# Streaming logsumexp: the last two tiles are loaded and computed by one written list

## The chip, the cores and the metric

The kernel runs on one core of one Trainium2 chip. The metric is the device time of one execution in microseconds; the median of three runs of the kernel before is 323.24. The profile pages and traces come from one profiled execution each. Engines are named as in the profile: PE (TensorE), DVE (VectorE), ACT (ScalarE), POOL (GpSimd) and SP (SyncE, which only issues transfers here).

## The reference

```python
# x: (8, 2048, 2048) float32, bias: (8, 256) float32
x_heads = x.reshape(B, S, H, Dh).transpose(0, 2, 1, 3) + bias[None, :, None, :]
x_tiled = np.repeat(x_heads, 2, axis=2)
mx = x_tiled.max(axis=-1, keepdims=True)
lse = mx.squeeze(-1) + np.log(np.exp(x_tiled - mx).sum(axis=-1))
```

So each row of 2048 numbers has 8 heads of 256. For each row and head the kernel needs log(sum(exp(x + bias))), and writes it twice. The input is 134 MB, the output 1 MB.

## The kernel before

The 16,384 rows are cut into 64 tiles of 128 partitions by 2 rows (K = 2), 2 MB each. Eight tile buffers stand in SBUF (four `xb` of two tiles). SP issues all loads of x and later three of the four stores; a load may also have to wait until the eighth transfer before it has landed, since eight semaphores are used in turn. No maximum is subtracted: the sums of exp(x + bias) are taken directly, and a range check at the end decides whether a second, slow pass with the maximum (`all_again`) is run.

There are three ways to bring the bias in:

- PE: a matmul writes the bias of a head into a PSUM bank (bf16, L343 and L360), a second one with an identity matrix adds x (float32, L378 in `add_x`, L401). ACT then takes exp from PSUM and sums it by its accumulator (`sum_biased`, L432).
- ACT takes exp(x) in place (`exp_inplace`, L457), and DVE multiplies by exp(bias) and sums in one instruction (`weigh`, L492).
- ACT takes exp(x), and POOL multiplies by exp(bias) and folds 256 columns to 32 by three additions (`fold`, L508 and L516); DVE reduces the rest (L522).

In the bulk (tiles 0 to 53) POOL adds the bias of the upper heads instead (L451) and DVE reduces with L476. `STAGES` says which heads go which way from which tile on. Tiles 57 to 61 have two heads on PE, five on DVE, one on POOL, for each row by itself. Tile 62 has one on PE, six on DVE and one on POOL in each row; tile 63 has two, four and two in its first row and three, five and none in its second. Tile 63 is loaded in pieces of columns (`LAST_COLS`), and two pieces of its second row by one transfer (`LAST_BOTH`).

Every engine runs its instructions in the written order (`tc.manual_schedule`). The loop writes for each unit: the x-add on PE, the next unit's bias matmul, warm matmuls that nobody reads (`keep_warm`, L392), the exp, then the previous unit's sums from PSUM, then the weighing. So the sums of a unit stand behind the exp of the next one on ACT.

The end: all sums of the last batch stand in the tile `R_last`. PE transposes it (L696), ACT takes the log (L702) and issues the store (L703). The range check looks at the float bits of all sums as integers. Per group of batches DVE takes a maximum and a minimum and hands them on to the next group (`ends_of`, `ends_of_last(0)`, L563 and L564, between tiles 61 and 62), at the end it does so for the rest (`ends_of_last(1)`), combines both (L608), PE turns the 128 partitions into one row (L602, L616), DVE reduces that row to one number (L617), and every engine loads it into a register (L620) and branches.

Of the kernel before, what the change touches and what calls it, by code (L numbers as in the profile page):

```python
# [17 lines left out]
K = 2  # L18
# [18 lines left out]
PROMPT_F2 = dict(pe=2, acc=2, g0=8, late=False, fold=2)  # L37
SINGLE_F1 = dict(pe=1, acc=1, g0=8, late=False, fold=1)
TRIPLE = dict(pe=3, acc=3, g0=8, late=False, fold=0)
# [12 lines left out]
    (62, (SINGLE_F1, SINGLE_F1)),  # L52
    (63, (PROMPT_F2, TRIPLE)),
]

LAST_COLS = [
    [(0, 512), (1280, 2048), (512, 1280)],
    [(0, 512), (768, 1280), (1280, 1792), (512, 768), (1792, 2048)],
]

LAST_BOTH = (512, 1792)
# [3 lines left out]
def kernel(  # L65
# [41 lines left out]
    one_bits = sb.tile([1, 1], BF16, name="one_bits")  # L107
    ends = sb.tile([P, 2], F32, name="ends")
    far = sb.tile([P, 1], BF16, name="far")
    verdict = sb.tile([1, 1], I32, name="verdict")  # L110

    NR = KB * H * NB
# [6 lines left out]
    pads = [1] * (len(widths) - 1) + [NBLK * K]  # L119
# [10 lines left out]
    R.append(sums_in[-2].rearrange("p (k h n) -> p k h n", k=K, h=H))  # L130
    R_last = sums_in[-1].rearrange("p (h n k) -> p h n k", h=H, n=NBLK)
# [19 lines left out]
    def pieces(t):  # L151

        if len(modes_of(t)) == 1:
            return [(0, K, 0, D)]
        cols = [[(0, D)]] * K if t < T - 1 else LAST_COLS
        return [(k, k + 1, c0, c1) for k in range(K) for c0, c1 in cols[k]]
# [35 lines left out]
    def load(t):  # L192
        if TB <= t < BLOCKS:

            if t % TB == 0:
                after = [u for i in range(TB) if t >= NBUF for u in last_uses[t + i - NBUF]]
                ins = on_x(
                    t,
                    nc.sync.dma_start(
                        out=xbs[t // TB % len(xbs)], in_=rows_of(t, TB)  # L200
                    ),
                    after,
                )
                for i in range(TB):
                    loads[t + i, 0, 0] = ins
            return
        after = last_uses[t - NBUF] if t >= NBUF else []
        for k0, k1, c0, c1 in pieces(t):
            if t == T - 1 and k0 == K - 1 and c0 in LAST_BOTH:
                if c0 == LAST_BOTH[0]:  # L210
                    both = slice(0, None, (LAST_BOTH[1] - c0) // Dh)
                    v = [
                        a[:, k0, c0:D].rearrange("p (a j) -> p a j", j=Dh)[:, both]
                        for a in (xts[t % NBUF], rows_of(t))
                    ]
                    ins = on_x(t, nc.sync.dma_start(out=v[0], in_=v[1]), after)
                    for c in LAST_BOTH:
                        loads[t, k0, c] = ins
                continue
            loads[t, k0, c0] = on_x(  # L220
                t,
                nc.sync.dma_start(
                    out=xts[t % NBUF][:, k0:k1, c0:c1],
                    in_=rows_of(t)[:, k0:k1, c0:c1],
                ),
                after,
            )

    def reload(t):

        n = t + NBUF
        if n < BLOCKS:
            if n % TB == TB - 1:
                load(n - TB + 1)
        elif n < T:
            load(n)

# [50 lines left out]
    nc.vector.memset(Rx[-1], 1.0)  # L288
    nc.vector.memset(one_bits, float(ONE_BITS))
# [32 lines left out]
    def on_bank(i, ins):  # L322
        for j, u in bank_users[i // 2]:
            if j != i and u.ins.engine != ins.ins.engine:
                tc.declare_no_dep(ins.ins, u.ins, reason="another bank")
        bank_users[i // 2].append((i, ins))
        return ins
# [176 lines left out]
    def fold(t, k, h0, h1, sums, after):  # L504


        v = xts[t % NBUF][:, k, h0 * Dh : h1 * Dh]
        done = nc.gpsimd.tensor_tensor(  # L508
            out=v, in0=v, in1=w_sb[:, h0 * Dh - W1 : h1 * Dh - W1], op=ALU.mult
        )  # L510
        on_x(t, done, [after])
        v = v.rearrange("p (h j) -> p h j", j=Dh)
        n = Dh
        while n > FOLD:
            n //= 2
            done = nc.gpsimd.tensor_tensor(  # L516
                out=v[:, :, 0:n], in0=v[:, :, 0:n], in1=v[:, :, n : 2 * n], op=ALU.add
            )
            on_x(t, done, [])

        def add_fold():
            red = nc.vector.tensor_reduce(  # L522
                out=sums[:, k, h0:h1],
                in_=v[:, :, 0:FOLD],
                op=ALU.add,
                axis=mybir.AxisListType.X,
            )
            on_x(t, red, [done])

        return add_fold  # L530
# [29 lines left out]
    def min_max(low_in, high_in, low, high, axis, last=False):  # L560


        nc.vector.tensor_reduce(out=high, in_=high_in, op=ALU.max, axis=axis)  # L563
        nc.vector.tensor_reduce(out=low, in_=low_in, op=ALU.min, axis=axis, negate=last)  # L564

    def ends_of(i):


        bits = Rx[i].bitcast(I32)
        at = pads[i + 1] + widths[i + 1]  # L570
        min_max(
            bits[:, 0 : 1 + widths[i]],
            bits[:, 1:],
            Rx[i + 1][:, 0:1].bitcast(I32),
            Rx[i + 1][:, at : at + 1].bitcast(I32),
            mybir.AxisListType.X,
        )

    def ends_of_last(half):


        bits = Rx[-1].bitcast(I32)
        n = NBLK * K
        c = half * n // 2
        views = [
            bass.AP(
                tensor=bits.tensor,
                offset=bits.offset + c0 + c,
                ap=[bits.ap[0], [n, H + 1], [1, n // 2]],
            )  # L590
            for c0 in (0, n)
        ]
        if half == 0:
            c = n // 2
            to = [bits[:, c0 + c : c0 + c + 1] for c0 in (0, n + NR)]
        else:
            to = [ends[:, 0:1], ends[:, 1:2]]
        min_max(*views, *to, mybir.AxisListType.XY, last=half == 1)

    def begin_row():  # L600
        row = one_ps[0:1, 0:P]
        nc.tensor.matmul(row, lhsT=one_bits, rhs=ones_bf[0:1], start=True, stop=False)  # L602
        return row

    def judge(row):


        nc.vector.scalar_tensor_tensor(  # L608
            out=far,
            in0=ends[:, 1:2],  # L610
            scalar=-2.0 * ONE_BITS,
            in1=ends[:, 0:1],
            op0=ALU.add,
            op1=ALU.max,
        )
        nc.tensor.matmul(row, lhsT=far, rhs=ident_bf, start=False, stop=True)  # L616
        nc.vector.tensor_reduce(  # L617
            out=verdict, in_=row, op=ALU.max, axis=mybir.AxisListType.X
        )
        return nc.values_load(  # L620
            verdict,
            min_val=0,
            max_val=(1 << 31) - 1,
            skip_runtime_bounds_check_because="it is only compared, and addresses nothing",
        )

    def all_again():
# [10 lines left out]
        with tc.For_i(0, B, 1) as b, tc.For_i(0, S // P, 1) as n:  # L638
# [28 lines left out]
            nc.sync.dma_start(  # L667
# [41 lines left out]
    def sums_of(t):  # L709
# [16 lines left out]
        for t in range(T)  # L726
        for k0, k1, c0, _ in pieces(t)
        if c0 == 0
# [8 lines left out]
    for t in range(T):  # L737
# [4 lines left out]
        for k0, k1, c0, c1 in pieces(t):  # L742
# [3 lines left out]
            if c0 == 0:  # L746
                bias_here = bias_there
# [9 lines left out]
            if c0 == 0:  # L757
                if next_units and not m["late"]:
                    bias_there = put_bias(*next_units.pop(0))
                if t > T_PROMPT and m["g0"] == H:  # L760
                    keep_warm()
                if m["g0"] < H:
                    add = g_add(m, t, k0, k1)
                wait_for_pool = t == T_ROWS and k0 == 0
                if (t < T - 1 or k0 == 0) and not wait_for_pool:
                    flush(for_pool)
            h0 = max(c0 // Dh, m["pe"])
            h1 = min(c1 // Dh, m["g0"])
            hf = max(h0, min(h1, H - m["fold"]))
# [8 lines left out]
            if c0 == 0:  # L778
                flush(for_pe)
# [18 lines left out]
            if m["g0"] < H:  # L798
                pe_part()
                if t == T_PROMPT - 1:  # L800
                    first_factors()
                if m["late"]:
                    bias_there = put_bias(*next_units.pop(0))
            elif heads:
                for_pe.append(pe_part)
# [14 lines left out]
    flush(for_pe)  # L820
    flush(for_pool)
    finish_last()
    ends_of_last(1)
    again = judge(row) > SPAN_BITS
# [34 lines left out]
```

## Time and profile before

| | us |
|---|---|
| runs | 323.17, 323.24, 323.34 |
| the profiled execution | 323.2 |
| its span, first to last instruction | 321.3 |
| DVE busy | 287.8 (90%) |
| POOL busy | 288.2 (90%) |
| ACT busy | 264.4 (82%) |
| PE busy | 247.4 (77%) |
| moved by DMA | 135.44 MB, mean 422 GB/s |

The span is what the trace covers; the rest of the time lies around it. A row of the timeline gives the start, the length, the engine, the line of the kernel, the operation with output and input, and in brackets how long the engine was idle before it and what ended that. Engines overlap the end of one instruction with the start of the next, so costs in a row are read from start to start. A float32 matmul shows as two passes (x2).

### The profile page before, as it was taken

The page shows a single profiled execution, that of the slowest core. Times are in us where ns is not written, and L with a number is a line of the kernel's source. Part 1 is how long each engine was busy: PE and PEld are TensorE (multiplying, and loading weights), DVE is VectorE, ACT ScalarE, POOL GpSimd, SP SyncE. Part 2 cuts the span into 40 slices and gives each one's busy share as a digit, 9 for nine tenths or more (in the row PEclk, how much of TensorE's full clock was granted, in tenths as well). Part 3 has the DMA queues.
Part 4 walks back from the last instruction along what each step waited for, and adds up shares of the span by engine and source line. Part 5 has one row for each costly group of instructions (what it writes and reads, how often), then busy time and mean ns, then how long its engine had stood idle before and what let it go on. Part 6 is the DMA issues. An engine that isn't in the chain of part 4 may idle for free.

```text
span 321.3 us, 2277 instructions
## 1 busy us (share of the span) xinstructions
PE 247.4 (77%) x609; PEld 99.3 (31%) x610; DVE 287.8 (90%) x313; ACT 264.4 (82%) x434; POOL 288.2 (90%) x121
## 2 busy tenths in 40 slices
PE   4998885877886667887877876877877688688874
PEld 1333332323332223333323322332332233133331
DVE  1437999799989999969999999899999999999996
ACT  1159987798688888599789988889888998999995
POOL 6949998999999999999999999999999999978774
PEclk9979996899799999598999998999999999799999
DMA  7999999999999999999999999999999999999994
GB/s 297 455 424 453 416 438 443 404 457 432 416 457 413 432 451 412 441 445 408 450 438 420 445 414 436 424 428 428 439 434 426 425 424 446 415 424 429 428 410 183
DMA packets 8790, 135.44 MB, mean 422 GB/s; under 512 B 964, under 2 KB 1351, under 8 KB 2375
## 3 DMA queue, kind: packets, MB, share of 16 engines
q1 hardware_dynamic: 8624, 135.14, 98.3%
q10 hardware_dynamic: 152, 0.14, 0.1%
q8 instruction: 5, 0.08, 0.1%
q14 instruction: 9, 0.07, 0.1%
HBM read 134.23 MB, written 1.05 MB: 421 GB/s over the span
## 4 chain that ended last, share of the span: by engine, by line
DMA 48%; DVE 29%; PE 9%; ACT 8%; POOL 4%; issue 0%; SPq 0%; DVEq 0%
DMA xb<-in_x_dram 48%; DVE R L476 23%; ACT xb L457 5%; POOL xb L451 4%; DVE xb L469 4%; PE pair L401 4%; PE one_ps L401 2%; DVE xb L492 2%; PE pair L274 1%; ACT xb L419 1%; PE pair L343 1%; DMA brow<-in_bias_dram 1%; PE one_ps L343 1%; ACT xb L412 0%; PE w_ps L274 0%
## 5 line engine op out<-in xcount | busy, mean ns | idle before, releaser
L451 POOL TENSOR_TENSOR xb<-xb,b_rep 128x2048 f32<-128x2048 f32 x57 | 257.6, 4544 | 18.4 <-DMA xb<-in_x_dram 18.3
L476 DVE TENSOR_REDUCE R<-xb 128x14 f32<-128x3584 f32 (+1 forms) x57 | 216.8, 3803 | 2.6 <-ACT xb L457 0.7
L457 ACT ACTIVATE xb<-xb 128x2560 f32<-128x2560 f32 (+7 forms) x77 | 156.2, 2040 | 19.2 <-POOL xb L451 18.8
L401 PE MATMUL pair<-xb,ident 128*128 128x512 f32 x216 | 109.8, 634 | 0.0
L401 PE MATMUL one_ps<-xb,ident 128*128 128x512 f32 x108 | 62.9, 667 | 16.8 <-DMA xb<-in_x_dram 16.8
L419 ACT ACTIVATE xb<-pair 128x1024 f32<-128x1024 f32 x54 | 55.5, 1028 | 17.2 <-PE pair L401 17.1
L401 PEld LDWEIGHTS pair<-xb,ident 128*128 128x128 f32 x216 | 44.7, 207 | 58.7 <-issue 58.7
L469 DVE TENSOR_TENSOR xb<-xb,w_ps 128x512 f32<-128x512 f32 x54 | 36.7, 680 | 20.4 <-ACT xb L457 20.3
L343 PE MATMUL one_ps<-b,ones_bf 128*128 128x512 bf16 x52 | 19.9, 382 | 38.4 <-ACT xb L412 38.4
L412 ACT ACTIVATE xb<-one_ps 128x256 f32<-128x256 f32 x108 | 39.9, 378 | 7.0 <-PE one_ps L401 7.0
L343 PEld LDWEIGHTS <-ones_bf 128*128 128x128 bf16 (+1 forms) x174 | 17.4, 101 | 86.3 <-issue 79.3
L343 PE MATMUL pair<-b,ones_bf 128*128 128x512 bf16 x104 | 31.0, 379 | 0.0
L378 PE MATMUL pair<-xb,ident 128*128 128x512 f32 (+1 forms) x42 | 22.7, 636 | 9.5 <-DMA xb<-in_x_dram 9.5
L401 PEld LDWEIGHTS one_ps<-xb,ident 128*128 128x128 f32 x108 | 19.8, 200 | 31.5 <-DMA xb<-in_x_dram 25.3
L492 DVE CUSTOM_DVE_ANT_0 xb<-xb,w_ps 128x256 f32<-128x256 f32 x61 | 22.3, 416 | 0.0
L412 ACT ACTIVATION_READ_ACCUMULATOR xb<-one_ps 128x1 f32 x108 | 22.0, 204 | 0.0
L516 POOL TENSOR_TENSOR xb<-xb 128x128 f32<-128x128 f32 (+3 forms) x39 | 13.9, 356 | 3.1
L432 ACT ACTIVATE xb<-pair 128x256 f32<-128x256 f32 x39 | 14.7, 401 | 0.0
L508 POOL TENSOR_TENSOR xb<-xb,w_sb 128x256 f32<-128x256 f32 (+1 forms) x13 | 10.0, 772 | 4.9 <-ACT xb L457 4.4
L378 PEld LDWEIGHTS pair<-xb,ident 128*128 128x128 f32 x42 | 6.9, 195 | 21.2 <-DMA xb<-in_x_dram 19.2
L392 PE MATMUL tp<-b_rep,ident 128*128 128x384 f32 x28 | 11.3, 486 | 0.0
L492 DVE CUSTOM_DVE_ANT_0 xb<-xb,one_ps 128x256 f32<-128x256 f32 x21 | 8.5, 414 | 0.4 <-ACT xb L457 0.2
(61 smaller groups left out, 73.8 us busy)
## 6 DMA issues: line engine op xcount, KB each, us to landing
xb<-in_x_dram SPq DMA_DIRECT2D x20, 4096.0 KB, 21.9
xb<-in_x_dram SPq DMA_DIRECT2D x17, 2048.0 KB, 22.2
xb<-in_x_dram SPq DMA_DIRECT2D x12, 1024.0 KB, 22.3
xb<-in_x_dram SPq DMA_DIRECT2D x5, 256.0 KB, 11.1
xb<-in_x_dram SPq DMA_DIRECT2D x2, 384.0 KB, 15.6
out_dram<-res SPq DMA_DIRECT2D x1, 512.0 KB, 6.4
out_dram<-res SPq DMA_DIRECT2D x1, 256.0 KB
out_dram<-res_two SPq DMA_DIRECT2D x1, 128.0 KB, 5.7
```

Of the source, the lines that this page charges most:

```text
L343: nc.tensor.matmul(p, lhsT=lhsT, rhs=each_row(b, h * Dh, Dh, K), start=i == 0, stop=False,)
L378: mm = nc.tensor.matmul(p, lhsT=ident, rhs=xts[t % NBUF][:, ka:kb, c : c + w], start=False, stop=True,)
L401: mm = nc.tensor.matmul(p, lhsT=ident, rhs=xts[t % NBUF][:, :, h * Dh : (h + 1) * Dh], start=False, stop=True,)
L412: act = nc.scalar.activation(out=xts[t % NBUF][:, k, 0:Dh], in_=got[0][:, k * Dh : (k + 1) * Dh], func=ACT.Exp, accum_out=sums[:, k, 0:1],)
L419: act = nc.scalar.activation(out=xts[t % NBUF][:, :, Dh : m["pe"] * Dh].rearrange("p k (h j) -> p h k j", j=Dh), in_=got[-1].rearrange("p ...
L432: act = nc.scalar.activation(out=xts[t % NBUF][:, k, h * Dh : (h + 1) * Dh], in_=p, func=ACT.Exp, accum_out=sums[:, k, h : h + 1],)
L451: add = nc.gpsimd.tensor_tensor(out=v, in0=v, in1=each_row(b_rep, c - G0, D - c, k1 - k0), op=ALU.add)
L457: return on_x(t, nc.scalar.activation(out=v, in_=v, func=ACT.Exp), [after])
L469: mul = nc.vector.tensor_tensor(out=f, in0=f, in1=each_row(w_ps, m["pe"] * Dh - W0, n, k1 - k0), op=ALU.mult,)
L476: red = nc.vector.tensor_reduce(out=sums[:, k0:k1, h0:H], in_=v.rearrange("p k (h j) -> p k h j", j=Dh), op=ALU.add, axis=mybir.AxisListTy ...
L492: ttr = nc.vector.tensor_tensor_reduce(out=v, in0=v, in1=w, scale=1.0, scalar=0.0, op0=ALU.mult, op1=ALU.add, accum_out=dst,)
L516: done = nc.gpsimd.tensor_tensor(out=v[:, :, 0:n], in0=v[:, :, 0:n], in1=v[:, :, n : 2 * n], op=ALU.add)
```

## The change

Tiles 62 and 63 leave the stages and the loop. Their four rows get names: a and b are the rows of tile 62, c and d those of tile 63. A list (`TAIL_LOADS`) says which heads of which row each of ten transfers brings, and a second list (`TAIL`) writes the work on them in order, one word for each instruction: `add` (x onto the bias in PSUM, and the bias matmul of the next `add` behind it), `warm`, `exp`, `weigh`, `sum` (exp from PSUM with the accumulator), `copy` (exp of three heads from PSUM to SBUF, no sum), `halves` (DVE adds the two halves of such a head and sums, 128 elements), `fold` by single steps and `folded`. The sums of tile 61 (`sums`) stand ahead of the first exp of row a. The exps are 256 to 1280 elements for 256 to 1792 before.

The range check changes: POOL subtracts the bits of 1.0 from all sums that are known by tile 61 (`bits`), DVE reduces their absolute values to one number for each partition (`limit`), and at the end DVE does the same for the 32 last columns, with that number beside them; a matmul by a column of 2^-8 adds up the 128 partitions, and one element is copied. A constant column with the limit itself makes the sum exceed half the limit only if a partition does. In `all_again` a store is issued by ACT instead of SP.

```diff
-    (62, (SINGLE_F1, SINGLE_F1)),
-    (63, (PROMPT_F2, TRIPLE)),
 ]
+T_TAIL = 62
+TAIL_LOADS = [
+    (62, 0, 0, 8),
+    (62, 1, 4, 8),
+    (63, 0, 3, 8),
+    (63, 1, 4, 8),
+    (63, 0, 0, 1),
+    (62, 1, 2, 4),
+    (62, 1, 0, 2),
+    (63, 0, 1, 3),
+    (63, 1, 2, 4),
+    (63, 1, 0, 2),
+]
+ROWS = {"a": (62, 0), "b": (62, 1), "c": (63, 0), "d": (63, 1)}
+TAIL = """
+add a:01  sums  add a:2  warm  warm
+exp a:3-5  exp a:67
+weigh a:3  rest  weigh a:4  weigh a:5  weigh a:6  weigh a:7
+bits
+exp b:4-7
+fold b:67.0
+weigh b:4  weigh b:5
+copy a:012
+halves a:0  halves a:1  halves a:2
+exp c:3-7
+fold b:67.1
+limit
+add c:0  warm
+weigh c:3  weigh c:4
+exp d:4-7
+fold c:67.0
+weigh c:5
+add b:2
+exp b:3
+weigh d:4
+sum c:0
+weigh d:5
+add b:0  warm
+exp b:1
+fold c:67.1
+weigh d:6
+sum b:2
+add c:1  warm
+weigh d:7
+exp c:2
+fold b:67.2
+weigh b:3
+sum b:0
+add d:2
+weigh b:1
+exp d:3
+fold c:67.2
+weigh c:2
+sum c:1
+add d:0
+exp d:1
+weigh d:3
+fold b:67.3
+sum d:2
+weigh d:1
+fold c:67.3
+folded b:67
+sum d:0
+folded c:67
+"""
...
+    def next_bias():
...
+        p = ps[bank][:, 0:n]
+        mm = nc.tensor.matmul(
+            p, lhsT=ones_bf, rhs=each_row(b3, heads[0] * Dh, n, 1), start=True, stop=False
+        )
...
+        if what == "add":
+            bank, c = biased[(t, k), heads[0]]
+            mm = nc.tensor.matmul(in_ps(bank, c, n), lhsT=ident, rhs=v, start=False, stop=True)
+            on_bank(bank, on_x(t, mm, [loads[t, k, heads[0] * Dh]]))
...
+            next_bias()
...
+        if what == "copy":
+            bank, c = biased[(t, k), heads[0]]
+            act = nc.scalar.activation(out=v, in_=in_ps(bank, c, n), func=ACT.Exp)
...
+        if what == "halves":
+            (h,) = heads
+            ttr = nc.vector.tensor_tensor_reduce(
+                out=v[:, 0 : Dh // 2],
+                in0=v[:, 0 : Dh // 2],
+                in1=v[:, Dh // 2 :],
...
+                accum_out=dst,
+            )
...
+    def off_one(engine, to, bits):
+        engine.tensor_scalar(
+            out=to,
+            in0=bits,
+            scalar1=-1.0 * ONE_BITS,
+            scalar2=None,
+            op0=ALU.add,
+        )
...
+    def off_seen():
+        n = 1 + 2 + NR
+        off_one(nc.gpsimd, off[:, 1:n], Rx[len(groups)].bitcast(I32))
+        to = off[:, n:].rearrange("p (h c) -> p h c", h=H)
+        off_one(nc.gpsimd, to, last_bits(0, SEEN))
...
+    def limit_seen():
+        n = H * LATE
+        farthest(off_last[:, n : n + 1], off)
+
+    def judge():
+        n = H * LATE
+        to = off_last[:, 0:n].rearrange("p (h c) -> p h c", h=H)
+        off_one(nc.vector, to, last_bits(SEEN, NBLK * K))
+        farthest(far, off_last)
+        total = tp[0:1, 0, 0:1]
+        nc.tensor.matmul(total, lhsT=far, rhs=scale_bf, start=True, stop=True)
+        nc.vector.tensor_copy(verdict, total)
...
-            ends_of(len(groups))
-            ends_of_last(0)
             store()
-    row = begin_row()
-    flush(for_pe)
-    flush(for_pool)
+    for what, row, heads, step in tail:
...
+        tail_step(what, *row, heads, step)
     finish_last()
-    ends_of_last(1)
-    again = judge(row) > SPAN_BITS
+    again = judge() > SPAN_BITS // 2
```

More of the change, by code (lines that the diff above doesn't have):

```diff
@@ L106 @@
     ident_bf = sb.tile([P, P], BF16, name="ident_bf")
-    one_bits = sb.tile([1, 1], BF16, name="one_bits")
-    ends = sb.tile([P, 2], F32, name="ends")
+    NR = KB * H * NB
+    SEEN = (T_TAIL - (B - 1) * NBLK) * K
+    LATE = NBLK * K - SEEN
+    off = sb.tile([P, 1 + 2 + NR + H * SEEN], F32, name="off")
+    off_last = sb.tile([P, H * LATE + 1], F32, name="off_last")
     far = sb.tile([P, 1], BF16, name="far")
+    scale_bf = sb.tile([P, 1], BF16, name="scale_bf")
     verdict = sb.tile([1, 1], I32, name="verdict")
-    NR = KB * H * NB
     starts = [0]
@@ L154, in pieces @@
             return [(0, K, 0, D)]
-        cols = [[(0, D)]] * K if t < T - 1 else LAST_COLS
-        return [(k, k + 1, c0, c1) for k in range(K) for c0, c1 in cols[k]]
+        return [(k, k + 1, 0, D) for k in range(K)]
     def rows_of(t, n=1):
@@ L208, in load, with load_part, load_tail @@
         for k0, k1, c0, c1 in pieces(t):
[L209 to L227, printed above, removed]
+            loads[t, k0, c0] = load_part(t, k0, k1, c0, c1, after)
+    def load_part(t, k0, k1, c0, c1, after):
+        return on_x(
+            t,
+            nc.sync.dma_start(
+                out=xts[t % NBUF][:, k0:k1, c0:c1],
+                in_=rows_of(t)[:, k0:k1, c0:c1],
+            ),
+            after,
+        )
+    def load_tail():
+        for t, k, h0, h1 in TAIL_LOADS:
+            ins = load_part(t, k, k + 1, h0 * Dh, h1 * Dh, last_uses[t - NBUF])
+            for h in range(h0, h1):
+                loads[t, k, h * Dh] = ins
     def reload(t):
@@ L320, with on_bank @@
     bank_users = [[], []]
-    def on_bank(i, ins):
-        for j, u in bank_users[i // 2]:
-            if j != i and u.ins.engine != ins.ins.engine:
+    def on_bank(i, ins, banks=1):
+        here = range(i, i + banks)
+        for at, u in bank_users[i // 2]:
+            if not set(at) & set(here) and u.ins.engine != ins.ins.engine:
                 tc.declare_no_dep(ins.ins, u.ins, reason="another bank")
-        bank_users[i // 2].append((i, ins))
+        bank_users[i // 2].append((here, ins))
         return ins
@@ L502, in weigh, with fold_step, add_folded @@
         last_uses[t].append(on_x(t, ttr, [after]))
-    def fold(t, k, h0, h1, sums, after):
[L507 to L530, printed above, removed]
+    def fold_step(t, k, h0, h1, step, after):
+        v = xts[t % NBUF][:, k, h0 * Dh : h1 * Dh]
+        if step == 0:
+            done = nc.gpsimd.tensor_tensor(
+                out=v, in0=v, in1=w_sb[:, h0 * Dh - W1 : h1 * Dh - W1], op=ALU.mult
+            )
+            return on_x(t, done, [after])
+        v = v.rearrange("p (h j) -> p h j", j=Dh)
+        n = Dh >> step
+        done = nc.gpsimd.tensor_tensor(
+            out=v[:, :, 0:n], in0=v[:, :, 0:n], in1=v[:, :, n : 2 * n], op=ALU.add
+        )
+        return on_x(t, done, [])
+    def add_folded(t, k, h0, h1, sums, done):
+        v = xts[t % NBUF][:, k, h0 * Dh : h1 * Dh]
+        red = nc.vector.tensor_reduce(
+            out=sums[:, k, h0:h1],
+            in_=v.rearrange("p (h j) -> p h j", j=Dh)[:, :, 0:FOLD],
+            op=ALU.add,
+            axis=mybir.AxisListType.X,
+        )
+        on_x(t, red, [done])
+    def fold(t, k, h0, h1, sums, after):
+        step = 0
+        while Dh >> step >= FOLD:
+            after = fold_step(t, k, h0, h1, step, after)
+            step += 1
+        return lambda: add_folded(t, k, h0, h1, sums, after)
     def finish(i):
@@ L570, in ends_of @@
         at = pads[i + 1] + widths[i + 1]
[L571 to L576, printed above, removed]
-        )
[L579 to L614, printed above, removed]
-        )
[L616 to L619, printed above, removed]
+        for op, there, c in ((ALU.max, bits[:, 1:], at), (ALU.min, bits[:, 0 : 1 + widths[i]], 0)):
+            nc.vector.tensor_reduce(
+                out=Rx[i + 1][:, c : c + 1].bitcast(I32),
+                in_=there,
+                op=op,
+                axis=mybir.AxisListType.X,
+            )
@@ new lines, in farthest @@
+    def farthest(to, of):
+        nc.vector.tensor_reduce(
+            out=to,
+            in_=of,
+            op=ALU.max,
+            axis=mybir.AxisListType.X,
+            apply_absolute_value=True,
+        )
+    def limit_seen():
[9 more added lines that the diff above has]
+        nc.vector.tensor_copy(verdict, total)
@@ L666, in all_again @@
                 )
-            nc.sync.dma_start(
+            nc.scalar.dma_start(
                 out=outs[at].rearrange("b n p h r -> (b n p) h r"), in_=both
@@ L725 @@
         (modes_of(t)[k0], k0, k1)
-        for t in range(T)
-        for k0, k1, c0, _ in pieces(t)
-        if c0 == 0
+        for t in range(T_TAIL)
+        for k0, k1, _, _ in pieces(t)
     ]
@@ L735, in flush @@
         later_work.clear()
-    for t in range(T):
+    tail = []
+    for word in TAIL.replace("  ", "\n").split("\n"):
+        if not word.strip():
+            continue
+        what, _, of = word.strip().partition(" ")
+        row, _, heads = of.partition(":")
+        heads, _, step = heads.partition(".")
+        if "-" in heads:
+            heads = [h for h in range(int(heads[0]), int(heads[-1]) + 1)]
+        else:
+            heads = [int(h) for h in heads]
+        tail.append((what, ROWS.get(row), heads, int(step or 0)))
@@ new lines @@
+    to_bias = [(row, heads) for what, row, heads, _ in tail if what == "add"]
+    biased = {}
+    made = {}
+    def next_bias():
+        if not to_bias:
+            return
+        row, heads = to_bias.pop(0)
+        if len(heads) > 1:
+            n_ps[0] += n_ps[0] % 2
+        bank = n_ps[0] % len(ps)
+        n_ps[0] += 1
+        n = len(heads) * Dh
+        p = ps[bank][:, 0:n]
+        mm = nc.tensor.matmul(
+            p, lhsT=ones_bf, rhs=each_row(b3, heads[0] * Dh, n, 1), start=True, stop=False
+        )
+        on_bank(bank, mm)
+        for i, h in enumerate(heads):
+            biased[row, h] = (bank, i * Dh)
@@ new lines, in span_of, with in_ps, tail_step @@
+    def span_of(t, k, heads):
+        return xts[t % NBUF][:, k, heads[0] * Dh : (heads[-1] + 1) * Dh]
+    def in_ps(bank, c, n):
+        return pairs[bank // 2][:, bank % 2 * MM + c : bank % 2 * MM + c + n]
+    def tail_step(what, t, k, heads, step):
+        sums = sums_of(t)
+        n = len(heads) * Dh
+        v = span_of(t, k, heads)
+        dst = sums[:, k, heads[0] : heads[0] + 1]
+        if what == "add":
+            bank, c = biased[(t, k), heads[0]]
+            mm = nc.tensor.matmul(in_ps(bank, c, n), lhsT=ident, rhs=v, start=False, stop=True)
+            on_bank(bank, on_x(t, mm, [loads[t, k, heads[0] * Dh]]))
+            for h in heads:
+                made["add", t, k, h] = mm
+            next_bias()
+        if what == "sum":
+            (h,) = heads
+            bank, c = biased[(t, k), h]
+            sum_biased(t, k, h, bank, in_ps(bank, c, Dh), made["add", t, k, h], sums)
+        if what == "copy":
+            bank, c = biased[(t, k), heads[0]]
+            act = nc.scalar.activation(out=v, in_=in_ps(bank, c, n), func=ACT.Exp)
+            mms = [made["add", t, k, h] for h in heads]
+            on_bank(bank, on_x(t, act, mms), banks=(c + n + MM - 1) // MM)
+            for h in heads:
+                made["exp", t, k, h] = act
+        if what == "exp":
+            act = exp_inplace(t, v, loads[t, k, heads[0] * Dh])
+            for h in heads:
+                made["exp", t, k, h] = act
+        if what == "weigh":
+            (h,) = heads
+            weigh(t, v, h, dst, made["exp", t, k, h])
+        if what == "halves":
+            (h,) = heads
+            ttr = nc.vector.tensor_tensor_reduce(
+                out=v[:, 0 : Dh // 2],
+                in0=v[:, 0 : Dh // 2],
+                in1=v[:, Dh // 2 :],
+                scale=1.0,
+                scalar=0.0,
+                op0=ALU.add,
+                op1=ALU.add,
+                accum_out=dst,
+            )
+            on_x(t, ttr, [made["exp", t, k, h]])
+        if what == "fold":
+            after = made["exp", t, k, heads[0]] if step == 0 else None
+            done = fold_step(t, k, heads[0], heads[-1] + 1, step, after)
+            made["fold", t, k, heads[0]] = done
+        if what == "folded":
+            add_folded(t, k, heads[0], heads[-1] + 1, sums, made["fold", t, k, heads[0]])
@@ L738 @@
+    for t in range(T_TAIL):
         if t == T_FACTORS:
@@ L755, in pe_part @@
                         sum_biased(t, k, h, bank, p, mm, sums)
-            if c0 == 0:
-                if next_units and not m["late"]:
+            if not m["late"]:
+                if next_units:
                     bias_there = put_bias(*next_units.pop(0))
[L760 to L765, printed above, removed]
-                    flush(for_pool)
-            h0 = max(c0 // Dh, m["pe"])
-            h1 = min(c1 // Dh, m["g0"])
-            hf = max(h0, min(h1, H - m["fold"]))
+                else:
+                    next_bias()
+            if t > T_PROMPT and m["g0"] == H:
+                keep_warm()
+            if m["g0"] < H:
+                add = g_add(m, t, k0, k1)
+            wait_for_pool = t == T_ROWS and k0 == 0
+            if not wait_for_pool:
+                flush(for_pool)
+            h0 = m["pe"]
+            h1 = m["g0"]
+            hf = min(h1, H - m["fold"])
             if h0 < h1 and not m["late"]:
@@ L803 @@
                     bias_there = put_bias(*next_units.pop(0))
-            elif heads:
+            else:
                 for_pe.append(pe_part)
@@ L815 @@
         if t == T - 3:
-            ends_of(len(groups))
-            ends_of_last(0)
             store()
-    row = begin_row()
-    flush(for_pe)
-    flush(for_pool)
+    for what, row, heads, step in tail:
+        if row is None:
+            {
+                "sums": lambda: flush(for_pe),
+                "rest": lambda: flush(for_pool),
+                "bits": off_seen,
+                "limit": limit_seen,
+                "warm": keep_warm,
+            }[what]()
+            continue
+        tail_step(what, *row, heads, step)
     finish_last()
-    ends_of_last(1)
-    again = judge(row) > SPAN_BITS
+    again = judge() > SPAN_BITS // 2
     order.__exit__(None, None, None)
```

28 lines of the change are left out of this document (11 added, 17 removed).

## The prediction

> **What bounds the kernel now.** I read the page's bars by slice first, then the chain of waits, then the timeline of the last 18 us, since the change touches only tiles 62 and 63.
>
> ```profile
> DMA  7999999999999999999999999999999999999994
> GB/s 297 455 424 453 416 438 443 404 457 432 416 457 413 432 451 412 441 445 408 450 438 420 445 414 436 424 428 428 439 434 426 425 424 446 415 424 429 428 410 183
> ```
>
> The DMA engines are full in every slice but the first and last. So the input's arrival sets the time up to its last byte, and only what follows can be won or lost. The end of the chain of waits (start, length, what):
>
> ```profile
> 288.19 19.83 DMA xb<-in_x_dram
> 308.02 0.02 issue
> 308.05 1.70 ACT xb L457
> ...
> 310.49 1.71 ACT xb L457
> ...
> 312.22 0.42 DVE xb L492
> ...
> 317.56 0.14 DVE R L522
> ...
> 318.67 0.28 DVE verdict L617
> ```
>
> ScalarE's long exps of tile 62 release VectorE, which is then busy without a gap from 312.22 to 317.7. The timeline adds TensorE and the way out:
>
> ```profile
> 308.60 0.27 PE L360 MATMUL pair<-b,ones_bf 128*128 128x256 bf16 x1
> 308.71 0.81 PE L392 MATMUL tp<-b_rep,ident 128*128 128x384 f32 x2
> 310.51 0.70 PE L378 MATMUL pair<-xb,ident 128*128 128x256 f32 x2 [0.99 <-DMA xb<-in_x_dram]
> 313.09 0.81 PE L392 MATMUL tp<-b_rep,ident 128*128 128x384 f32 x2
> 313.74 1.04 PE L378 MATMUL pair<-xb,ident 128*128 128x512 f32 x2
> 315.65 0.70 PE L378 MATMUL pair<-xb,ident 128*128 128x256 f32 x2 [0.22 <-DMA xb<-in_x_dram]
> 317.31 0.24 ACT L432 ACTIVATION_READ_ACCUMULATOR xb<-pair 128x1 f32 x1
> 317.84 0.30 PE L696 MATMUL pair<-ident,R 128*128 128x128 f32 x1 [1.36 <-DVE R L522]
> 318.18 0.38 ACT L702 ACTIVATE res_last<-pair 128x256 f32<-128x256 f32 x1 [0.63 <-PE pair L696]
> 318.59 0.39 ACTq L703 DMA_DIRECT2D out_dram<-res_last  x1
> out_dram<-res_last ACTq DMA_DIRECT2D x1, 128.0 KB, 1.7
> ```
>
> Two ways lead from the last sum (VectorE 317.70, ScalarE 317.55) to the end. The verdict is written at 318.95, and the register loads that follow it (L620, 0.48 to 0.58 us) are over at 319.57. The output goes by transpose, Ln and transfer and lands at 318.59 + 1.7 = 320.3, 1.0 before the span's end at 321.3. The chain of waits shows the verdict, but the output lands later. So I take the end to follow the output, that is, the transpose, whose weights load at 317.81.
>
> **The change, part by part.** Durations are start-to-start in this stretch.
>
> *Loads.* Still 4 MB, as 10 transfers for 9. SyncE issues each when the eighth before it has landed, so the last is issued when row b's upper half lands (about 309.3, now 308.04) for a landing at 315.6: 6 us ahead, no gap in the queue. Piece sizes lie between those of today, so I keep the last landing at 315.6 (315.65, L378). The three stores, past one more load on SyncE's queue, move by 0.3 to 0.5 us; they land 5.7 to 6.4 us after issue, by 318.1, under the 320.3 above. The new order lands a whole at 308.03 (TensorE starts at 308.07), then b:4-7, c:3-7 and d:4-7. c:0 ends 1.75 MB after a. At the 2.44 us per MB between 308.07 and 310.51 that is 312.3; at the mean of the last 3 MB (7.58 us) it is 312.45. I take 312.4.
>
> *ScalarE.* A sum from PSUM takes 0.357 (L432, 309.65 to 310.00), an exp 0.09 us + 0.843 ns an element (L457: 1792 in 1.60, 768 in 0.73). The list puts tile 61's last two sums ahead of the exps of row a, partly into an idle 0.22, and has six later sums for seven, with three heads copied by one exp. From 307.73: 2 sums 0.71; exps of 768, 512 and 1024, the copy of 768, exps of 1280 and 1024: 5.07; five exps of 256: 1.53; six sums: 2.14. Total 9.46, so the engine, if it never waits, is done at 317.2 and its last sum is stored at 317.3 (now 317.55).
>
> *VectorE.* It weighs row a from 309.31 (exp a:3-5 ready) where it now starts on tile 62 at 309.77, and does 19 weighs for 21 at 0.342 (L492) = 6.50. Three "halves" of 128 elements are not in the trace: at least 0.21 (the 256 row less 128 elements at 1.04 ns, the clock at which the 129- and 72-element reduces differ), at most 0.342; I take 0.21, nearest in form. "limit" over 227 elements 0.31 (129: 0.20), three folded reduces 0.10 to 0.14. That is 7.8, or 317.1; it waits for exp d:1 and ends at 317.5. The four reduces of the range check between tiles 61 and 62 (L563, L564, 308.85 to 309.51) go; VectorE sits idle there until 309.31 instead. Even with 0.342 it ends 317.6.
>
> *POOL.* "bits" is two scalar additions of 130 and 96 elements, not in the trace: 0.25 to 0.46 each by L516's 32- and 128-element rows; I take 0.40. Then two folds of 512 (L508 1.30 each, L516 0.76, 0.49, 0.35) end at 316.6, ahead of the reduces at 317.2. Covered by VectorE's queue.
>
> *TensorE, where the new wait is.* An add of 256 takes 0.43 (0.535 where it waited for its load: 308.07 to 308.60), a bias matmul 0.108 (308.60 to 308.71), a warm matmul 0.645 (313.09 to 313.74). After c:0 the list asks, in this order: add c:0, bias, warm; add b:2, bias; add b:0, bias, warm; add c:1, bias, warm; add d:2, bias; add d:0. The engine runs in order, and three warms stand between adds that ScalarE needs. From 312.4: 0.535 + 0.108 + 0.645, 0.427 + 0.108, 0.427 + 0.108 + 0.645, 0.427 + 0.108 + 0.645, 0.427 + 0.108, 0.59 to the last result = 5.31, so d:0 is ready at 317.71, though its bytes landed at 315.6. ScalarE could start that sum 0.7 earlier; it waits for c:1 (0.1), for d:2 (0.45) and for d:0 (0.15). The last sum runs 317.74 to 318.22. Queued behind it are the transpose, the Ln and the output.
>
> *Range check.* After the last sum: 0.18 + 0.18 (reduce rows of 32), a one-column matmul of at most 0.22 (L616), a copy of 0.15 to 0.28, waits 0.15: about 0.85 to 1.0 for 1.26 now. It is covered by the output transfer and worth nothing by itself; without that cover it would be 0.3.
>
> *The rest.* A 128x160 memset less and two small ones more at the start lie under the first loads; the store in the second pass over the input (only after a failed range check) moves to ScalarE's queue and doesn't run.
>
> *Sum.* The transpose's weights load at 318.25 for 317.81: +0.44; no wait for VectorE's semaphore stands ahead of it now, and the drain at the end checks that transfer one place later (-0.05). Span 321.3 + 0.4 = 321.7. The profiled execution took 323.2, 1.9 over its span, and the median of the runs is 323.24. So **323.65**, +0.13%. The same sums laid out for the kernel before give the transpose at 317.77 (317.81 in the trace).
>
> *A rule against it.* The granted clock falls to half at times: 273.00 to 276.41 has TensorE busy 0.98 of 3.41 us, and 276.41 to 279.82 then runs at 0.50. Cut into such stretches, the trace has seven at full clock that were at most half busy, all followed by 0.50, and of the busier ones one, at 17.0 in the start-up. In the new list the emptiest 3.4 us of the tail (311.0 idle to 312.4) is 63% busy, so I charge nothing. [...]
>
> **The rivals.**
> 1. *The adds keep up* (c:0 lands by 311.8, or warms slip beside waits). Then ScalarE's 317.3 and VectorE's 317.5 decide, the transpose loads at 317.45: -0.4, 322.85. For it: ScalarE is packed and everything else has slack. Against: TensorE's rows are exact and the queue's rate is steady. 22%.
> 2. *The chain is later still*: each 0.1 in c:0's landing is 0.1 at the end. From 312.65 on it is over +0.65 (324.0). The smaller pieces of the queue or one more stall on a PSUM bank would do it. 14%.
> 3. *POOL's bits are slow.* The operand is integer, and no such row exists. From 1.2 us each they decide: the folds start late, and VectorE's reduces with them; at 2.0 each POOL ends at 319.0, the transpose at 319.3: +1.5, 324.75. Against: a cast of 768 takes 0.81. 6%.
> 4. *The clock halves* in 314 to 317.4: the chain's 3.4 us do half their work, +1.7, 324.9. Against: the 63%. 4%.
> 5. *The change does not do what it says*: the one-column check and the pairwise sums shorten work that nobody waits for, and other stalls cancel: 323.2. It is the middle between forecast and rival 1. 8%.
>
> **How the numbers follow.** The forecast has 46%. The range reaches from rival 1 with 0.25 more (322.6) to rival 2 and most of the way to 3 and 4 (324.5). The likeliest's own range is 323.4 to 323.9, c:0 landing between 312.15 and 312.65. 0.2% is 0.65 us, about what a measurement of this kernel can tell from no change. Slower: rivals 2 to 4 and 2% of the unknown, 0.26. Faster: the far end of rival 1, 0.10. Within: 0.64.
>
> **What would show it.** Right: ScalarE idle for about 0.6 us in all before its last two sums, ended by the adds; the add of d:0 starting at 317.1 without a wait for DMA; c:0's add at 312.4; VectorE waiting for ScalarE at the end; verdict at about 319.05. Wrong: the last sum following the one before by 0.36 with no wait (rival 1), the folded reduces waiting for POOL (3), a granted clock of 0.5 before 317.4 (4), or a last landing other than 315.6.

## The result and the profile after

| | before | after |
|---|---|---|
| median of 6 runs, us | 323.21 | 325.56 |
| lowest and highest run | 323.08, 324.23 | 325.51, 325.82 |
| span of the profiled execution | 321.3 | 323.7 |
| row a has landed | 308.02 | 309.69 |
| last input has landed | 315.60 | 317.50 |
| last output has landed | 320.32 | 322.72 |

The ratio is 1.0069, 95% interval 1.0056 to 1.0082: the changed kernel is 2.35 us slower, where 0.4 was forecast. The table already says where to look. Row a is the first transfer of the changed list and brings the same bytes as before, behind 62 tiles whose loads are unchanged, and it is 1.67 late. So most of the loss is there before the tail begins.

The page of the changed kernel: the DMA engines' busy tenths, the rate by slice, the packets, and the loading queue (packets, MB, share of 16 engines' span).

```profile
DMA  7999999999999999999999999999999999999993
GB/s 309 470 397 445 454 401 440 445 409 441 445 409 442 441 407 441 441 413 438 445 410 441 441 411 441 413 427 427 433 429 422 429 424 426 419 421 419 419 399 145
DMA packets 8806, 135.44 MB, mean 418 GB/s; under 512 B 980, under 2 KB 1239, under 8 KB 2519
q1 hardware_dynamic: 8640, 135.14, 98.2%
```

The packets and the same queue before:

```profile
DMA packets 8790, 135.44 MB, mean 422 GB/s; under 512 B 964, under 2 KB 1351, under 8 KB 2375
q1 hardware_dynamic: 8624, 135.14, 98.3%
```

The engines are as full as before, for a longer span: by the packet records the loading queue holds each engine for 317.7 us (98.2% of 323.7) against 315.9 (98.3% of 321.3). So no gap has opened in the queue. The same bytes need 1.8 us more of the engines.

The end of the chain of waits after (start, length, what):

```profile
299.82 14.39 DMA xb<-in_x_dram
314.21 0.04 issue
314.26 0.70 PE pair L846 x2
...
317.98 0.65 PE tp L455 x2
318.63 0.43 PE pair L846 x2
319.06 0.11 PE pair L826
319.17 0.45 PE pair L846 x2
319.62 0.02 issue
319.64 0.48 ACT xb L495 x2
...
320.81 0.15 DVE verdict L681
```

From the landing of c:0 at 314.21 TensorE's adds and warms run without a gap to 319.62, 5.41 us; the forecast had this chain with 5.31, from a landing at 312.4. The timeline of the same end:

```profile
317.91 0.38 ACT L495 ACTIVATE xb<-pair 128x256 f32<-128x256 f32 x1 [0.28 <-PE pair L846]
319.10 0.38 ACT L495 ACTIVATE xb<-pair 128x256 f32<-128x256 f32 x1 [0.41 <-PE pair L846]
319.37 0.33 DVE L585 TENSOR_REDUCE R<-xb 128x2 f32<-128x64 f32 x2
320.17 0.33 PE L758 MATMUL pair<-ident,R 128*128 128x128 f32 x1 [0.56 <-ACT xb L495]
320.95 0.39 ACTq L765 DMA_DIRECT2D out_dram<-res_last  x1
```

ScalarE waits for the add of c:1 (0.28 idle, 0.1 forecast) and for that of d:2 (0.41, 0.45 forecast); its last sum, d:0, starts 0.54 after the sum of d:2 instead of 0.36, so it waits about 0.18 (0.15 forecast). The forecast's sign, about 0.6 idle before the last two sums, is there. The transpose waits for ScalarE. The tail has the forecast's shape, moved by 1.9 us. What moved it is outside the stretch that the prediction worked on.

### The profile page after: what moved, and what is told of

It reads as the page before. It is cut to its first block, busy times and chain, and to the rows that moved or that the text cites. A ratio compares the mean times of both kernels' runs of the same rounds, so it can differ in the third digit from the quotient of the medians.

```text
span 323.7 us, 2296 instructions
## 1 busy us (share of the span) xinstructions
PE 247.5 (76%) x619; PEld 100.1 (31%) x620; DVE 288.0 (89%) x310; ACT 265.6 (82%) x436; POOL 287.9 (89%) x119
## 3 DMA queue, kind: packets, MB, share of 16 engines
q1 hardware_dynamic: 8640, 135.14, 98.2%
## 4 chain that ended last, share of the span: by engine, by line
DMA 58%; POOL 18%; ACT 14%; PE 5%; DVE 3%; SPq 1%; issue 0%
DMA xb<-in_x_dram 58%; POOL xb L514 18%; ACT xb L520 9%; DVE R L539 2%; PE pair L464 2%; ACT xb L495 2%; ACT xb L482 1%; PE one_ps L464 1%; ACT xb L475 1%; PE pair L846 1%; PE tp L455 1%; SPq L261 1%; DVE xb L532 0%; SPq L276 0%; PE pair L826 0%
## 5 line engine op out<-in xcount | busy, mean ns | idle before, releaser
L520 ACT ACTIVATE xb<-xb 128x2560 f32<-128x2560 f32 (+5 forms) x80 | 156.2, 1965 | 20.1 <-POOL xb L514 19.5
L464 PE MATMUL pair<-xb,ident 128*128 128x512 f32 x216 | 108.2, 625 | 0.0
L464 PEld LDWEIGHTS pair<-xb,ident 128*128 128x128 f32 x216 | 44.1, 204 | 58.1 <-issue 58.1
L441 PE MATMUL pair<-xb,ident 128*128 128x512 f32 x32 | 18.6, 684 | 8.5 <-DMA xb<-in_x_dram 8.5
L455 PE MATMUL tp<-b_rep,ident 128*128 128x384 f32 x30 | 12.0, 486 | 0.0
L441 PEld LDWEIGHTS pair<-xb,ident 128*128 128x128 f32 x32 | 5.3, 197 | 17.7 <-DMA xb<-in_x_dram 15.9
L495 ACT ACTIVATION_READ_ACCUMULATOR xb<-pair 128x1 f32 x38 | 8.4, 220 | 0.0
```

What stands on the lines that cost most here:

```text
L441: mm = nc.tensor.matmul(p, lhsT=ident, rhs=xts[t % NBUF][:, ka:kb, c : c + w], start=False, stop=True,)
L455: nc.tensor.matmul(tp[:, 0 : WARM // P], lhsT=ident, rhs=b_rep[:, 0:WARM], start=True, stop=True)
L464: mm = nc.tensor.matmul(p, lhsT=ident, rhs=xts[t % NBUF][:, :, h * Dh : (h + 1) * Dh], start=False, stop=True,)
L495: act = nc.scalar.activation(out=xts[t % NBUF][:, k, h * Dh : (h + 1) * Dh], in_=p, func=ACT.Exp, accum_out=sums[:, k, h : h + 1],)
L520: return on_x(t, nc.scalar.activation(out=v, in_=v, func=ACT.Exp), [after])
```

## The experiments

### Where the input buffers stand

The diff adds small tiles ahead of the input buffers (`off`, `off_last`, `scale_bf`) and drops others. In the built program the buffers `xb` start at byte 60416 of each partition before, and at 61344 after. The first is 236 times 256, the second is a multiple of 32 only. The first pair of kernels tries this address alone, both ways round. In the changed kernel, an unused tile ahead of the buffers moves them to 61440 = 240 times 256:

```diff
+    spare = sb.tile([P, 24], F32, name="spare")
```

> The changed kernel, with 96 unused bytes in each partition ahead of the input buffers, so that they start at byte 61440 (a multiple of 1024, as 60416 was before) and no longer at 61344; nothing else differs. Theory A (the loads are slower since the input buffers moved to an address that is no multiple of 64): row a lands at 308.0 as before, for 309.7 in the changed kernel; then only the tail's loss is left, span 321.7 to 321.9, time 323.6 to 323.8. Theory B (something else of the change slows the loads over the whole run: the memsets at the start, the order of issues, later releases of buffers): nothing moves, row a at 309.7, span 323.7, time 325.5.

In the kernel before, one of 232 columns moves them to 61344:

```diff
+    spare = sb.tile([P, 232], F32, name="spare")
```

> The kernel before, with 928 unused bytes ahead of the input buffers, which so start at byte 61344 as in the changed kernel; no instruction is added. Theory A (address): the load of row 62:0 lands at 309.7 for 308.0, 8192-byte packets take a mean of 0.314 us or so for 0.310, span 323.0, time 324.9. Theory B (something else of the change): 323.2, row at 308.0.

| kernel | xb at byte | median us | ratio to before, same chip | packet of 8192 B, mean ns | time of all packets / 16, us |
|---|---|---|---|---|---|
| before | 60416 | 323.11 (323.21 beside "after") | | 310.1 | 316.9 |
| after | 61344 | 325.56 | 1.0069 [1.0056, 1.0082] | 315.2 | 318.8 |
| after, moved | 61440 | 323.67 | 1.0011 [0.9999, 1.0023] | 310.3 | 317.0 |
| before, moved | 61344 | 325.18 | 1.0072 [1.0056, 1.0089] | 315.3 | 318.8 |

The last two columns are taken from the packet records of the traces. The old work with the new address has 2.07 us of the 2.35, and the new work with the old kind of address keeps only 0.56. In the moved kernel before, row a lands at 309.83 for 308.02; in the moved changed kernel it lands at 307.93. Theory A held both times, though its size for the moved kernel before, 324.9, was 0.3 too small. The page of the moved kernel before:

```profile
DMA packets 8790, 135.44 MB, mean 419 GB/s; under 512 B 964, under 2 KB 1351, under 8 KB 2375
q1 hardware_dynamic: 8624, 135.14, 98.3%
```

These are the packets of the kernel before, byte for byte, at 419 GB/s for 422. By size, moved against unmoved: 1806 packets of 8192 bytes took 5.2 ns more each, 2053 of 16384 bytes 3.5 more, 2560 of 32768 bytes 3.4 more, and the smaller ones 0.2 us on each engine in all. Shared by 16 engines, that is 0.59 + 0.45 + 0.54 + 0.22 = 1.80 us, for 1.9 between the spans of the two profiled executions and 2.07 in the medians. From 8192 bytes up the price is 3 to 5 ns a packet, not a share of its bytes.

What is left of the realigned kernel is the tail by itself, and here its timeline can be laid beside the forecast:

```profile
312.36 0.70 PE L847 MATMUL pair<-xb,ident 128*128 128x256 f32 x2 [1.31 <-DMA xb<-in_x_dram]
316.01 0.38 ACT L496 ACTIVATE xb<-pair 128x256 f32<-128x256 f32 x1 [0.24 <-PE pair L847]
317.20 0.39 ACT L496 ACTIVATE xb<-pair 128x256 f32<-128x256 f32 x1 [0.41 <-PE pair L847]
317.68 0.34 DVE L586 TENSOR_REDUCE R<-xb 128x2 f32<-128x64 f32 x2
318.27 0.33 PE L759 MATMUL pair<-ident,R 128*128 128x128 f32 x1 [0.56 <-ACT xb L496]
318.91 0.15 DVE L682 CAST verdict<-tp 1x1 int32<-1x1 f32 x1 [0.26 <-PE tp L681]
319.06 0.39 ACTq L766 DMA_DIRECT2D out_dram<-res_last  x1
```

Transpose at 318.27 (forecast 318.25), verdict at 319.06 (319.05), span 321.8 (321.7), time 323.67 (323.65). The last input lands at 315.52, for 315.6 in the forecast. Against the kernel before that was measured beside it the time is 0.56 longer, where 0.41 was forecast; the interval of the ratio, 0.9999 to 1.0023, just reaches 1, so the tail's own loss rests on the rows more than on the times.

### How fine the address counts

The same one-line edit in the kernel before, with 16, 32 and 64 columns (64, 128 and 256 bytes).

> The kernel before with the input buffers 64 bytes further on, at 60480 (a multiple of 64, not of 128). How fine the address matters: if a multiple of 64 is enough, 323.2; if 128 or more is needed, slower, by up to the 1.7 us that theory A gives to 61344, time up to 324.9. If the address is nothing (theory B), 323.2 here and in the shifted kernel.

> The kernel before with one unused tile of 32 columns ahead of the input buffers, so that these start at byte 60544, a multiple of 128 and not of 256. If what counts is a multiple of 256: 325.0 to 325.3 us, packets of 8192 bytes at 0.312 to 0.313 us. If a multiple of 128 is enough: 323.0 to 323.3 us, packets at 0.309.

> The kernel before with the input buffers 256 bytes further on, at 60672: a multiple of 256, not of 512. At 60480 (a multiple of 64) it took 325.1. If 256 is enough: 323.1, median packet of 8192 bytes 0.309 us; if not: 325.1, 0.313 us.

| xb at byte | multiple of | median us | ratio to before | packet of 8192 B, mean ns |
|---|---|---|---|---|
| 60480 | 64 | 325.08 | 1.0059 [1.0043, 1.0076] | 314.6 |
| 60544 | 128 | 325.21 | 1.0055 [1.0043, 1.0067] | 314.8 |
| 60672 | 256 | 323.16 | 1.0001 [0.9992, 1.0011] | 310.1 |

64 and 128 are not enough, 256 is. It is no matter of how far the buffers moved: 256 bytes cost nothing, 64 cost the whole (0.2 more than the 324.9 that was expected at most).

Against the 310.1 ns at 60416, packets of 8192 bytes took 4.5 ns more at 60480, 4.7 at 60544 and 5.2 at 61344, that is 64, 128 and 160 bytes past a multiple of 256; packets of 32768 bytes took 3.4 ns more at all three addresses. The loads read the same bytes of x as before, and only the address that they write to had moved. So the price hardly grows with the distance; what makes it up stays open.

### TensorE's chain

With the buffers in place, the tail can be taken apart. First the three warm matmuls between the adds go, the wait on which the forecast rests:

```diff
-add c:0  warm
+add c:0
...
-add b:0  warm
+add b:0
...
-add c:1  warm
+add c:1
```

> The changed kernel with the buffers at 61440, and without the three warm matmuls behind add c:0, add b:0 and add c:1. If the queue of adds on TensorE sets the end of the tail (chain theory): the adds follow their loads, ScalarE no longer waits and stores its last sum at about 317.4 for 318.3, span 320.9 to 321.1, time 322.8 to 323.0, that is 0.8 us under the realigned kernel with the warms. Rival (the last load or ScalarE's own queue sets it, the adds only seem to): within 0.2 us of the realigned kernel. Second rival (the warms keep TensorE's clock up): the granted clock falls to 0.5 before 317 and it is slower than with them.

323.50 us, ratio 1.0012 [1.0002, 1.0021]: 0.17 less than with the warms, where the theory of the chain had promised much more. The chain itself did go; the timeline shows no wait of ScalarE for TensorE, and ScalarE was done at 317.29. But:

```profile
311.83 0.68 DVE L872 CUSTOM_DVE_ANT_0 xb<-xb 128x128 f32<-128x128 f32 x1
312.44 0.28 DVE L872 CUSTOM_DVE_ANT_0 xb<-xb 128x128 f32<-128x128 f32 x1
312.65 0.81 DVE L872 CUSTOM_DVE_ANT_0 xb<-xb 128x128 f32<-128x128 f32 x1
315.66 0.69 PE L847 MATMUL pair<-xb,ident 128*128 128x256 f32 x2
317.79 0.34 DVE L586 TENSOR_REDUCE R<-xb 128x2 f32<-128x64 f32 x2
318.27 0.30 PE L759 MATMUL pair<-ident,R 128*128 128x128 f32 x1 [1.92 <-DVE R L586]
```

The add of d:0 starts at 315.66, behind its load (landed at 315.60), and the transpose still starts at 318.27: now it waits for VectorE's last reduces, which end at 318.13. VectorE lost its time in the "halves". Three instructions of one shape take 0.68, 0.28 and 0.81. POOL's rows beside them, and just ahead of its multiply VectorE's weigh of a:7, whose factors lie in SBUF (`w_sb`) and not in PSUM:

```profile
310.80 0.42 DVE L556 CUSTOM_DVE_ANT_0 xb<-xb,w_sb 128x256 f32<-128x256 f32 x1
310.85 1.50 POOL L573 TENSOR_TENSOR xb<-xb,w_sb 128x512 f32<-128x512 f32 x1 [0.37 <-ACT xb L521]
312.43 0.88 POOL L579 TENSOR_TENSOR xb<-xb 128x256 f32<-128x256 f32 x1
313.26 1.33 POOL L573 TENSOR_TENSOR xb<-xb,w_sb 128x512 f32<-128x512 f32 x1
```

The long halves end at 312.51 and 313.46, 0.15 behind the ends of POOL's multiply (312.35) and of its first fold (313.31), and the second half starts as that fold does. That looks like waiting for the other engine to finish an instruction. No semaphore says so: in the trace it is only a longer instruction.

### The halves

Two kernels test it, both without the three warms. One forms the same three sums by one reduce, which has one input; the other keeps the halves and leaves out POOL's multiplies and folds in the tail, so that four of its sums are of unweighted, unfolded data:

```diff
-halves a:0  halves a:1  halves a:2
+reduce a:012
...
+        if what == "reduce":
+            red = nc.vector.tensor_reduce(
+                out=sums[:, k, heads[0] : heads[-1] + 1],
+                in_=v.rearrange("p (h j) -> p h j", j=Dh),
+                op=ALU.add,
+                axis=mybir.AxisListType.X,
+            )
```

> Realigned buffers, the three warms gone, and the three pairwise sums of row a (two inputs from SBUF each, 0.66 + 0.28 + 0.81 us in the trace for the 0.21 each that was assumed) replaced by one reduce of 128x768 with one input (0.87 by the slope of the reduce rows). Lock theory (a VectorE instruction with two inputs from SBUF and a POOL instruction that reads SBUF wait for each other): the reduce takes 0.87 beside POOL's folds, VectorE ends 0.6 to 0.7 earlier, at 317.5, behind ScalarE's 317.3; the transpose loads at 317.6, span 321.0 to 321.1, time 322.8 to 322.9, under the kernel before. Rival (summing those heads is slow on VectorE in any form beside POOL): the reduce takes 1.5, time 323.5 as without the warms.

```diff
-fold b:67.0
...
-fold c:67.3
```

> Realigned buffers, no warms, pairwise sums kept; the eight steps by which POOL weighs and folds heads 6 and 7 of rows b and c are left out, so those four sums are of unweighted, unfolded data. Lock theory: with POOL still, each pairwise sum takes 0.28 (0.21 from start to start), VectorE ends near 317.4, time 322.8. Rival (the pairwise sum is slow by itself, or by the ports of its own engine): 0.66 and 0.81 stay, time 323.5.

The third has the reduce and keeps the warms:

> Realigned buffers, the warms kept, the one reduce in place of the pairwise sums. Chain theory: TensorE's adds still end the tail, d:0 ready at 317.7, so VectorE's gain is hidden: time 323.6 as in the realigned kernel, span 321.8. Rival (the pairwise sums alone cost the tail its time, and the warms nothing): 322.9.

The halves with POOL silent:

```profile
311.84 0.29 DVE L864 CUSTOM_DVE_ANT_0 xb<-xb 128x128 f32<-128x128 f32 x1
...
312.05 0.29 DVE L864 CUSTOM_DVE_ANT_0 xb<-xb 128x128 f32<-128x128 f32 x1
...
312.26 0.29 DVE L864 CUSTOM_DVE_ANT_0 xb<-xb 128x128 f32<-128x128 f32 x1
```

Start to start that is 0.21 each, the price of the forecast, and 322.67 us, 0.998 [0.997, 0.9989]. The reduce, in the kernel with POOL at work:

```profile
310.79 1.50 POOL L573 TENSOR_TENSOR xb<-xb,w_sb 128x512 f32<-128x512 f32 x1 [0.37 <-ACT xb L521]
311.76 0.95 DVE L884 TENSOR_REDUCE R<-xb 128x3 f32<-128x768 f32 x1
312.37 0.73 POOL L579 TENSOR_TENSOR xb<-xb 128x256 f32<-128x256 f32 x1
```

It runs across POOL's multiply and fold in 0.95, 0.87 to the next start, and the fold is back at 0.73 for 0.88: the halves had slowed POOL too. POOL's multiply stays at 1.50, while its second multiply of the same shape takes 1.28 in this kernel: the weigh of a:7, with both inputs in SBUF, starts 0.06 ahead of the first. So the rows read as if the one that starts second waits, whichever engine it is; no run takes that weigh away. The lengths are what the rows show: 0.68 and 0.81 for the halves beside POOL's instructions against 0.29 with POOL silent, and 0.95 for the reduce beside them. What ties the two engines together they do not show.

With the buffers in place, the two edits make a square (medians, us; in brackets the difference to the kernel before, which took 323.11 beside the upper row and 323.18 beside the lower):

| | warms kept | warms gone |
|---|---|---|
| halves | 323.67 (+0.56) | 323.50 (+0.39) |
| one reduce | 323.58 (+0.40) | 322.90 (-0.28) |

By the differences either alone gives 0.16 or 0.17, and both give 0.84. With the reduce and the warms, the wait is back on TensorE:

```profile
317.28 0.38 ACT L496 ACTIVATE xb<-pair 128x256 f32<-128x256 f32 x1 [0.41 <-PE pair L847]
318.33 0.18 DVE L643 TENSOR_SCALAR off_last<-R 128x32 f32<-128x32 int32 x1 [0.74 <-ACT xb L496]
```

VectorE stands idle for 0.74 there, which is the gain of the reduce, unused. The kernel with both edits is the fastest here that computes all sums: ratio 0.9993 [0.9984, 1.0002], 0.28 under the kernel before in the medians. The interval reaches past 1, so a gain is likely and not shown.

## Why the prediction missed, point by point

**The step that failed** is the one on the loads: "Piece sizes lie between those of today, so I keep the last landing at 315.6". It counted bytes, transfers and their order, took the rate from the trace of before, and did not ask where the bytes go. The last input landed at 317.50. New tiles ahead of the buffers moved these off a multiple of 256, and the packets of 8192 bytes and more paid 3 to 5 ns each, over the whole run. That is 1.8 to 1.9 us of the 2.35 by the packets' times. Moving the buffers back takes away 1.79, with the last landing at 315.52, and leaves 0.56 for the tail, where 0.41 was forecast. So the step was right for buffers that stay at a multiple of 256. A last landing other than 315.6 was among the forecast's signs of being wrong, without a price. The prediction said itself that the DMA engines are full and that "the input's arrival sets the time up to its last byte"; so a change of the rate by 0.6% outweighs the whole effect that was forecast for the tail. It had no rival for it, and its range ended at 324.5.

**The chain of the adds** was right, and its size too: 5.41 against 5.31, from a landing of c:0 at 312.31 against 312.4 with the buffers in place. The two errors cancel, so the match of the transpose to 0.02 is partly luck.

**ScalarE** was right: done at 317.29 where nothing holds it, 317.3 forecast.

**VectorE's halves** were mis-sized: 0.21 each, at most 0.342, and start to start they took 0.59, 0.21 and 0.74 in the changed kernel, 1.54 for 0.63. The bounds came from rows with one input in SBUF; the one weigh of the kernel before in that stretch with both there (317.14, 0.42) met only the last 0.1 us of a fold of POOL's. VectorE's last reduces were therefore at 318.0 in the realigned kernel and not at 317.5, which cost nothing as long as TensorE's chain put ScalarE's last sum at 318.2. It also means that the first rival, in which the adds keep up and 322.85 results, was priced on the same too-short halves: without the chain the time was 323.50, and only with both edits 322.90.

**POOL's "bits"** took 0.55 and 0.46 for 0.40 each, the first over its bound of 0.46, and stayed covered. The rival of a slow "bits" fell, and so did the halved clock: the granted clock was 1.00 from 307.5 to the last matmul. Without the three warms (and with the reduce) TensorE was busy 2.13 of the 3.40 us from 314.3 on and kept 1.00, so they were not needed for it here.

**The output sets the end**, not the verdict. From before to the realigned kernel the verdict's end moved by 0.11 (318.95 to 319.06), the issue of the output by 0.47 (318.59 to 319.06), its landing by 0.50 and the span by 0.5. The span ended 0.99 to 1.00 after that landing with the old ending and 0.96 after it with the new one, for which the forecast took off 0.05. That fits a shorter range check worth nothing, as forecast; a kernel that changes only the check was not tried.

## What to carry to other kernels

Where a kernel is bound by its loads, look at the address at which the buffers end up, not only at the code: small tiles allocated ahead of them can move them (928 bytes here), and the cost was spread so thinly (3 to 5 ns a packet) that no row of the tail shows it. A landing that comes late although nothing ahead of it was changed is the sign (309.69 for 308.02); the mean rate (418 GB/s for 422) and the time per packet size (315.2 ns for 310.1 at 8192 bytes) tell it from a gap in the queue. And when two engines end a tail within a few tenths of each other, take both away before concluding that either was free.

## What the runs showed that was not expected

- The kernel's time went with the SBUF address that its loads write to: 323.1 to 323.3 us with the kernel before at 60416 or 60672, 325.1 to 325.2 at 60480, 60544 or 61344.
- The price was per packet, 3.4 to 5.2 ns from 8192 to 32768 bytes, and nearly the same 64, 128 or 160 bytes past a multiple of 256.
- The halves that seem to wait for POOL show no wait in the trace, only a length: 0.81 us for a pairwise sum of 128 elements that took 0.29 with POOL silent.
